# Attention scores as three float32r products, and another order of weight splits at the second feed-forward's border

## Chip, cores, metric

The kernel runs on one core of a Trainium2 chip. The metric is device time in microseconds (us). Engines: TensorE (PE; its weight loads are shown apart, as PEld), VectorE (DVE), ScalarE (ACT), GpSimd (POOL) and SyncE (SP), which issues most DMAs.

## The reference

One residual block of a streaming encoder on 256 frames of width 1024, all in float32:

```python
h = rmsnorm(x, ffn1_pre_g)
x = x + 0.5 * rmsnorm(swiglu(h, ffn1_w_in, ffn1_w_down), ffn1_post_g)
h = rmsnorm(x, mix_pre_g)
q_a, f_a, i_a, g_a, q_b, k_b, v_b, f_b, gates = split(h @ w_in)
o_a = rmsnorm(hgrn2(q_a, f_a, i_a), hg_norm_g) * silu(g_a)   # gated linear recurrence
o_b = fox_attention(q_b, k_b, v_b, f_b + bias)               # 8 heads of 128, causal
y = sigmoid(gate_A) * (o_a @ w_branch_a) + sigmoid(gate_B) * (o_b @ w_branch_b)
x = x + rmsnorm(y @ w_out, mix_post_g)
x = x + rmsnorm(mem_attention(rmsnorm(x), rmsnorm(mem)) @ w_mo, mem_post_g)
x = x + 0.5 * rmsnorm(swiglu(rmsnorm(x, ffn2_pre_g), ffn2_w_in, ffn2_w_down), ffn2_post_g)
```

Attention's logit of frame t for frame s <= t is q.k / sqrt(128) plus the sum of the log forget gates between them, and a softmax runs over s.

## The kernel before

**Precision and weights.** Most products are taken in the type float32r. Each operand is kept as two parts: the high part is the value cast to float32r, the low part is the value less the high part. A product is then three matmuls into one PSUM tile: high by high, high by low, low by high. Weights come in units of 128 x 1024 float32 (512 KB). `load_split` (line 134) loads a unit into one of four `raw` buffers (queue SP, line 141), casts it on ScalarE (line 143, `hi`) and subtracts on VectorE (line 145, `lo`), into eight buffers each; the first two units of `i_a` and of the second feed-forward go to buffers of the tag `extra` and are called `w` in the profile. Data tiles have tags as well: `m4` (21 tiles of 128 x 1024), `extra` (4 of that size). PSUM has banks `acc` (4), `mm` (2) and `tr` (2).

**Order.** A scheduler puts the instructions of each engine in a fixed order from the program's order and dependences. Two helpers steer it: `after(i)` (line 96) places a block at high priority behind the i-th matmul of a log, and `issue_after` puts an instruction behind a given one on the same engine; it is an order, not a semaphore. `hold` names, for a weight unit, the instruction pair (one of ScalarE, one of VectorE) behind which its cast and subtraction go.

**Stages.** First feed-forward, the combined projection with the recurrence, attention, gates and branches, memory attention, second feed-forward. The 256 frames are two halves of 128 (h = 0, 1). Between two stages `post` (line 384) norms a half's output and adds it to the residual `xs`: square sums of two PSUM tiles on ScalarE (line 283), `root` on ScalarE (lines 303, 304), `step` on VectorE, two residual sums on VectorE (line 404). `half` (line 599) then transposes the half in eight blocks on TensorE (line 368, four blocks to a `tr` bank), and `gain_split` writes each block's high part on ScalarE (line 358) and low part on VectorE (line 359) and notes the pair in `evicted`.

**The second feed-forward's border** (lines 1231 to 1253). The memory attention's outputs come from `mem_out` (line 1206), each in a `tr` bank. The output projection `rows_proj` of unit `mo` runs for half 0, then `post` of half 0; then 30 matmuls for half 1, and in between, behind the 20th and the 24th of them (`L_MO = 19`), the transposes of half 0. The feed-forward starts with two chunks of four units on half 0, 24 matmuls of 512 columns each, blocks of activations in rising order, then second half (transposes behind matmul `L_F2 = 36`).

**The first border** (lines 609 to 624) is alike: units of `i_a` on half 0, their second chunk's splits held behind evictions.

**Attention.** Keys and queries are projected in two groups g of four heads, scaled on VectorE (line 889), kept as float32 tiles `kb_[g]` and `qb_[g]`. `fox_scores(h)` (line 950) goes behind the 13th matmul (`F_S = 12`) of the value projection. For h = 0 each head's score is 128 x 128, in a `tr` bank; for h = 1 it is 128 x 256, in `acc` banks. Each score is one float32 matmul in the program, and two instructions in the profile. The `extra` buffers hold, one after the other, the recurrence's tiles `early` and `qf`, the gates' bias rows `brow` (loaded by SP, line 1032) and transposed probabilities.

**The start.** `WARM = 7` matmuls of ones, 128 x 128 float32 and two instructions each, run on TensorE while the first operands are loaded (lines 571, 572). Then `act_first` (line 461) takes two chunks block by block, 12 matmuls a block.

Of the kernel before, what the change touches and what calls it, by code (L numbers as in the profile page):

```python
# [12 lines left out]
F32R = mybir.dt.float32r  # L13
I32 = mybir.dt.int32
AF = mybir.ActivationFunctionType
ALU = mybir.AluOpType
AX = mybir.AxisListType

P = 128
D = 1024  # L20
T = 256
# [16 lines left out]
L_IA = 40  # L38
L_WO = 20
L_MK = 76  # L40
L_MO = 19
L_F2 = 36
L_OA = (4, 24)
F_S = 12
# [10 lines left out]

HX = T + 2 * KB

WARM = 7

X_AT = 12  # L60

# [8 lines left out]
_AT = {}  # L70
# [8 lines left out]
def block_kernel(ctx: ExitStack, tc: tile.TileContext, wts, head_in, gf_in, x_in, mem_in, memT_in, cols, rows, fbias, masks, out):  # L79
    nc = tc.nc  # L80
    V, S, G, PE = nc.vector, nc.scalar, nc.gpsimd, nc.tensor

    cp = ctx.enter_context(tc.tile_pool(name="consts", bufs=1))
    wp = ctx.enter_context(tc.tile_pool(name="weights", bufs=4))
# [7 lines left out]
    def MM(*args, **kw):  # L92
        log.append(PE.matmul(*args, **kw).ins)  # L93
# [9 lines left out]
    def nm(s):  # L103
        count[0] += 1
        return f"{s}_{count[0]}"

    def m4(shape, dt=F32, n="m"):
        return mp.tile(shape, dt, tag="m4", name=nm(n))
# [7 lines left out]
    def mm():  # L116
        return pp.tile([P, 512], F32, tag="mm", name=nm("mm"), bufs=2)

    def trp():
        return pp.tile([P, 512], F32, tag="tr", name=nm("tr"), bufs=2)  # L120
# [5 lines left out]
    evicted = []  # L126
    hold = {}
# [34 lines left out]
    def split(hi, lo, src):  # L162
        a = S.copy(hi, src)
        b = V.tensor_tensor(out=lo, in0=src, in1=hi.bitcast(F32), op=ALU.subtract)
        return a.ins, b.ins
# [124 lines left out]
    def sums_of(s, pre2=None):  # L290
# [5 lines left out]
            V.tensor_scalar(out=b, in0=s[:, 0:1], scalar1=pre2, scalar2=D * EPS, op0=ALU.mult, op1=ALU.add)  # L296
        return b

    def root(s, b, pre=None, pre2=None):

        sc = 1.0 if pre2 is None else pre2
        y, v = s1(name="y"), s1(name="v")
        S.activation(y, s[:, 1:2], AF.Abs_reciprocal_sqrt, bias=b, scale=sc)
        S.activation(v, s[:, 1:2], AF.Identity, bias=b, scale=sc)
        z = y
        if pre is not None:
            z = s1(name="z")
            S.activation(z, y, AF.Copy, scale=pre)
        return y, v, z

    def step(y, v, z):
# [25 lines left out]
    def fac_of(i, h):  # L337
        return fac[i][:, 32 * h : 32 * h + 1]
# [45 lines left out]
    def post(ps, h, grow, factor=1.0, pre=None, cuts=((0, 512), (512, 1024)), store=False):  # L384

        pre2 = None
        if pre is not None:
            pre2 = s1(name="pre2")
            V.tensor_tensor(out=pre2, in0=pre, in1=pre, op=ALU.mult)
        s = s1(2, name="ss2")  # L390
        ts = []
        for j in range(2):
            ssq(s[:, j : j + 1], ps[j])
            if j == 0:
                b = sums_of(s, pre2)
            else:
                y = root(s, b, pre, pre2)
            t = sp.tile([P, 512], F32, tag="z2", name=nm("post"), bufs=3)
            V.scalar_tensor_tensor(out=t, in0=ps[j], scalar=-factor * 16.0, in1=grow[:, j * 512 : (j + 1) * 512], op0=ALU.mult, op1=ALU.mult)  # L399
            ts.append(t)  # L400
        r = step(*y)
        for a, b in cuts:
            xh = xs[:, h, a:b]
            V.scalar_tensor_tensor(out=xh, in0=ts[a // 512][:, a % 512 : (b - 1) % 512 + 1], scalar=r, in1=xh, op0=ALU.mult, op1=ALU.add)  # L404
            if store:
                (nc.scalar if a in (320, 768) else nc.sync).dma_start(out[h * P : (h + 1) * P, a:b], xh)


    def ffn(w_in, w_dn, X, r2, n_tok, i_row, first_half, second_half=None):
# [146 lines left out]
    for kb in range(KB):  # L556
        heads.append(wp.tile([P, D], F32, tag="extra" if kb in (1, 2, 3, 4, 6) else "raw", name=nm("head"), bufs=4))
        n = HX if kb == 0 else 0
# [5 lines left out]
        if kb % 2 == 0 or kb == 1:  # L564
            a, b = ((0, 512), (512, D))[kb] if kb < 2 else (0, D)
# [4 lines left out]
    one = nc.const_aps.tensor(1.0, (P, P), F32)  # L570
    for _ in range(WARM):
        MM(wps[:, :P], one, one, start=True, stop=True)
# [26 lines left out]
    def half(X, r, h, g, *ms, into=None, act=True):  # L599

        for i, m in enumerate(ms):
            with after(m):
                to_T(X, x_blocks(h), h, g, (i,) if len(ms) == 2 else (0, 1))
        r[h] = rstd_x(x_halves(h), into, act)
# [7 lines left out]
    for h in range(2):  # L612
        m = len(log)
        for c in range(2):
            ps = mm()
            if h == 0 and c == 1:
                for i in range(4):
                    hold[_AT["i_a"] + 4 + i] = evicted[-1 if i else -3]
            u = chunk("i_a", c)
            proj_tok(ps, X2, u, h)  # L620
            iv_last = S.activation(iv[c][:, h, :], ps, AF.Copy, scale=r2[h]).ins
        if h == 0:
            half(X2, r2, 1, G_MIX, m + L_IA, into=fac_of(0, 1))
# [25 lines left out]
    for c in range(2):  # L649
        u = chunk("f_a", c)  # L650
        f, k = m4([P, 2, 4, P], n="f"), m4([P, 2, 4, P], n="k")
        for j in range(2):
            fj = heads_of(f, j)
            for i in (2 * j, 2 * j + 1):
                ps = acc()
# [10 lines left out]
    for c in range(2):  # L666
        u = chunk("q_a", c)
        q = m4([P, 2, 4, P], n="q")
        for j in range(2):
            qj = heads_of(q, j)  # L670
            z = sp.tile([P, 2, 2, P], F32, tag="z2", name=nm("z2"), bufs=3)
            for i in range(2):
                ps = acc()
# [162 lines left out]
    for c in range(3):  # L836
        u = [load_split(gf_in[4 * c + i], GF) for i in range(4)]
        n = min(GF, D - c * GF)
        for h in range(2):
            ps = mm()  # L840
# [32 lines left out]
    kb_, qb_, vb_ = [], [], []  # L873
    for c in range(2):
        for name, lst, sc in (("k_b", kb_, 1.0), ("q_b", qb_, 1.0 / math.sqrt(128.0))):
            u = chunk(name, c)
            t = m4([P, 4, T], n=name)
            m = len(log)
            for j in range(2):
                if c == 0:  # L880
                    ps = proj_col2(X2, u, (2 * j, 2 * j + 1))
                else:
                    for i, bank in enumerate((mm, trp)):
                        ps = bank()
                        proj_both(ps, X2, u, 2 * j + i)
                        added(t[:, 2 * j + i], ps)
                    ps = t[:, 2 * j : 2 * j + 2]
# [28 lines left out]
    ATs, A128s = [r.AT for r in recs], [r.A128 for r in recs]  # L916


    OA = Pair()
    for h in range(2):  # L920
        ps = [acc(), acc()]
        for hd in range(8):
            g, i = hd // 4, hd % 4
# [5 lines left out]
        r = rstd_x(ps)  # L929
# [10 lines left out]
    for g in range(2):  # L940
        t = m4([P, 4, T], n="cbm")
# [7 lines left out]

    def fox_scores(h):  # L950
        for g in range(2):
            k, q = kb_[g], qb_[g]
            ns = P * (h + 1)
            if h == 0:
                pv = trp().rearrange("p (i s) -> p i s", i=4)
                pv = [pv[:, i] for i in range(4)]
                p = sp.tile([P, 4, P], F32, tag="z2", name=nm("p0"), bufs=3)
            else:
                pv = score_psum()
                p = m4([P, 4, T], n="p1")  # L960
            mx, sm = s1(4, name="mx"), s1(4, name="sm")
            for i in range(4):
                MM(pv[i], q[:, i, h * P : (h + 1) * P], k[:, i, :ns], start=True, stop=True)
            for i in range(4):
                hd = 4 * g + i
                c1 = ct[:, h * 8 + hd : h * 8 + hd + 1]
                if h == 1:
                    V.scalar_tensor_tensor(out=p[:, i, 0:P], in0=pv[i][:, 0:P], scalar=c1, in1=cbc[:, hd], op0=ALU.add, op1=ALU.subtract)
                ds_ = slice(h * P, (h + 1) * P)
                V.scalar_tensor_tensor(out=p[:, i, ds_], in0=pv[i][:, ds_], scalar=c1, in1=cbm[g][:, i, ds_], op0=ALU.add, op1=ALU.subtract)  # L970
            V.tensor_reduce(out=mx, in_=p, axis=AX.X, op=ALU.max, negate=True)
            for i in range(4):
                S.activation(p[:, i], p[:, i], AF.Exp, bias=mx[:, i : i + 1], accum_out=sm[:, i : i + 1])
            V.reciprocal(sm, sm)
            V.tensor_tensor(out=p, in0=p, in1=bc(sm, [P, 4, ns], 2), op=ALU.mult)
            ps_[g, h] = p
# [34 lines left out]
    for c in range(2):  # L1011
        u = chunk("v_b", c)
        t = m4([P, 2, 512], n="v_b")
        for h in range(2):
            ps = mm()
# [25 lines left out]
    for h in range(2):  # L1041
        with after(m + L_OA[h]):
            to_T(OA, lambda kb: Gt[h][:, kb * P : (kb + 1) * P], h, G_HG)
    fox_pT(0, m + F_T[0])
# [38 lines left out]
    for c in range(2):  # L1083
        for name, X, zc in (("br_a", OA, c), ("br_b", OB, 2 + c)):
            u = chunk(name, c)
            for h in range(2):
                z = zs[zc][:, h]
                m = len(log)
                ps = mm()
# [21 lines left out]
    po = [[acc(), acc()], [acc(), acc()]]  # L1111
# [14 lines left out]
    for c in range(2):  # L1126
        u = chunk("mk", c)
        KM.more()
        for j in range(2):
            js = slice(2 * j, 2 * j + 2)  # L1130
            t = sp.tile([P, 2, T], F32, tag="z2", name=nm("km"), bufs=3)
            for i in range(2):
                ps = acc()
# [6 lines left out]
    for c in range(2):  # L1140
        u = chunk("mq", c)
        QM.more()
        for i in range(4):
            ps = acc()
# [3 lines left out]
            t = sp.tile([P, T], F32, tag="c1", name=nm("qm"), bufs=7)  # L1148
# [54 lines left out]
    g3 = load_row(2)  # L1203
    AO = Pair()

    def mem_out(i):
        ps = trp()
        for j in range(2):
            o = ps[:, j * T : (j + 1) * T]
            for sb in range(2):  # L1210

                n = sb * 512 + (2 * (i % 2) + j) * P
                vh = VM.h[i // 2][:, n // T, n % T : n % T + P]
                vl = VM.l[i // 2][:, n // T, n % T : n % T + P]
                MM(o, vh, pT.h[sb][:, i], start=(sb == 0), stop=False)
                MM(o, vl, pT.h[sb][:, i], start=False, stop=False)
                MM(o, vh, pT.l[sb][:, i], start=False, stop=(sb == 1))
        i2 = slice(2 * (i % 2), 2 * (i % 2) + 2)
        marks[2 + i] = split(AO.h[i // 2][:, i2], AO.l[i // 2][:, i2], ps.rearrange("p (a t) -> p a t", a=2))
# [17 lines left out]
    po = [[acc(), acc()], [acc(), acc()]]  # L1237
# [2 lines left out]
            rows_proj(po[h], AO, "mo", h, (kb,))  # L1240
    for n in range(2):
        rows_proj(po[0], AO, "mo", 0, range(3, KB), (n,))
    post(po[0], 0, g3)
    m = len(log)
    rows_proj(po[1], AO, "mo", 1, range(3, KB))
    half(X4, r4, 0, G_F2, m + L_MO, m + L_MO + 4, into=fac_of(3, 0))
    post(po[1], 1, g3)


# [95 lines left out]
```

## Time and profile before

| what | us |
|---|---|
| median of 3 runs | 787.14 |
| lowest, highest | 785.87, 789.0 |
| the profiled execution | 788.36 |
| its span, first to last instruction | 786.1 |
| VectorE busy in the span | 555.4 |
| ScalarE busy in the span | 462.8 |

A line of the profile reads: start and duration in us, engine, line of the kernel, operation, tile written <- tiles read, shape, number of merged instructions, and in brackets the engine's idle time before it with what ended it. A line of a tile's view gives the least, median and longest duration in ns, then the first and last start. A wait line gives the engine and tile that waited, what it waited for, the total in us, the number of times and the longest. A line of a window gives its borders and length, then busy time and number of instructions of each engine asked for, the granted clock, the DMA share and GB/s.

### The profile page before, as it was taken

To read this page: it belongs to the slowest core of one execution; us is meant where nothing else is said; L and a number is where in the kernel's file an instruction comes from. 1 tells how busy PE (TensorE), PEld (TensorE's weight loads), DVE (VectorE), ACT (ScalarE), POOL (GpSimd) and SP (SyncE) were. 2 spreads that over 40 slices of the span, in tenths; PEclk is the share of its full clock that TensorE was granted. 3 is DMA by queue.
4 is the path that set the end of the run, shared out by engine and by line. 5 is a ranking of instruction groups with operands and counts; after the bars stand their busy time and mean duration, and the time that the engine had idled before them with its cause. 6 is when DMAs were issued, how large, how long until landed. Compare 5 with 4: busy or idle time off the path is not lost.

```text
span 786.1 us, 12160 instructions
## 1 busy us (share of the span) xinstructions
PE 777.3 (99%) x4620; PEld 669.9 (85%) x4620; DVE 555.4 (71%) x895; ACT 462.8 (59%) x777; POOL 15.7 (2%) x39
## 2 busy tenths in 40 slices
PE   9999999999999999999999999999999999999996
PEld 7888888888888999898888888888887888888885
DVE  7766665586778899588676666885588566655563
ACT  7664544566765668467676345753667554544552
POOL 0000000000000102100000000000000000000000
PEclk9999999999999999999999999999999999999999
DMA  9665665463654546734576655465174546665431
GB/s 347 245 223 202 228 211 207 161 211 125 216 205 145 181 135 208 276 122 152 183 263 226 215 181 168 148 207 181 54 263 166 166 163 203 217 211 199 161 108 53
DMA packets 44505, 148.08 MB, mean 188 GB/s; under 512 B 5144, under 2 KB 8864, under 8 KB 44448
## 3 DMA queue, kind: packets, MB, share of 16 engines
q1 hardware_dynamic: 43168, 144.83, 53.5%
q0 software_dynamic: 848, 2.12, 1.1%
q8 instruction: 36, 0.59, 0.3%
q10 hardware_dynamic: 432, 0.37, 0.2%
q14 instruction: 21, 0.17, 0.1%
HBM read 146.24 MB, written 1.06 MB: 187 GB/s over the span
## 4 chain that ended last, share of the span: by engine, by line
PE 95%; DMA 2%; ACT 1%; DVE 1%; issue 0%; DVEq 0%; ACTq 0%
PE mm L93 43%; PE acc L93 37%; PE tr L93 13%; DMA raw<-in_wts_dram 2%; PE tr L368 1%; ACT hi L143 1%; DVE lo L145 0%; DMA head<-in_head_dram 0%; PE tr L985 0%; PE tr L426 0%; PE tr L1079 0%; PE acc L1198 0%; DVE xs L404 0%; ACT junk L283 0%; DVE post L399 0%
## 5 line engine op out<-in xcount | busy, mean ns | idle before, releaser
L145 DVE TENSOR_TENSOR lo<-raw,hi 128x1024 fp32r<-128x1024 f32 (+1 forms) x252 | 299.2, 1203 | 70.1 <-ACT hi L143 44.9
L143 ACT CAST hi<-raw 128x1024 fp32r<-128x1024 f32 (+1 forms) x252 | 254.9, 1037 | 68.0 <-PE mm L93 33.4
L93 PE MATMUL mm<-hi,hlT 128*128 128x512 f32 (+1 forms) x480 | 143.8, 379 | 0.0
L93 PE MATMUL acc<-hi,act 128*128 128x512 f32 x352 | 111.2, 390 | 0.0
L93 PEld LDWEIGHTS mm<-hi,hlT 128*128 128x128 f32 x480 | 88.1, 188 | 14.6 <-DVE hlT L359 0.3
L93 PE MATMUL mm<-hlT,hi 128*128 128x512 f32 (+1 forms) x432 | 99.5, 360 | 0.0
L93 PE MATMUL mm<-lo,hlT 128*128 128x512 f32 (+1 forms) x240 | 89.5, 378 | 0.0
L93 PEld LDWEIGHTS mm<-hlT,hi 128*128 128x128 f32 x432 | 75.5, 189 | 10.6
L93 PEld LDWEIGHTS acc<-hi,act 128*128 128x128 f32 x352 | 66.2, 188 | 13.4
L93 PE MATMUL tr<-hlT,hi 128*128 128x512 f32 x288 | 72.1, 392 | 0.0
L93 PE MATMUL acc<-lo,act 128*128 128x512 f32 x176 | 68.8, 391 | 0.0
L93 PE MATMUL acc<-hlT,hi 128*128 128x512 f32 x272 | 68.4, 393 | 0.0
L93 PE MATMUL mm<-hlT,lo 128*128 128x256 f32 x368 | 60.9, 283 | 0.0
L93 PEld LDWEIGHTS tr<-hlT,hi 128*128 128x128 f32 x288 | 51.8, 189 | 9.3
L93 PEld LDWEIGHTS acc<-hlT,hi 128*128 128x128 f32 x272 | 48.9, 189 | 8.8
L93 PEld LDWEIGHTS mm<-hlT,lo 128*128 128x128 f32 x368 | 53.7, 190 | 3.0
L93 PEld LDWEIGHTS mm<-lo,hlT 128*128 128x128 f32 x240 | 45.0, 188 | 7.0
L215 ACT COPY plo<-mm 128x256 f32<-128x256 f32 x38 | 14.1, 372 | 55.0 <-PE mm L93 55.0
L93 PEld LDWEIGHTS tr<-hlT,lo 128*128 128x128 f32 x288 | 39.3, 190 | 2.8
L93 PE MATMUL tr<-hlT,lo 128*128 128x256 f32 x288 | 40.2, 282 | 0.0
L93 PEld LDWEIGHTS acc<-hlT,lo 128*128 128x128 f32 x272 | 37.3, 190 | 2.7
L93 PE MATMUL acc<-hlT,lo 128*128 128x256 f32 x272 | 38.6, 283 | 0.0
(245 smaller groups left out, 1002.1 us busy)
## 6 DMA issues: line engine op xcount, KB each, us to landing
raw<-in_wts_dram SPq DMA_DIRECT2D x247, 512.0 KB, 4.5
raw<-in_gf_dram SPq DMA_DIRECT2D x12, 344.0 KB, 3.9
head<-in_head_dram SPq DMA_DIRECT2D x7, 392.0 KB, 6.6
grow<-in_rows_dram SPq DMA_DIRECT2D x4, 512.0 KB, 6.9
xs<-in_x_dram SPq DMA_DIRECT2D x2, 512.0 KB, 7.7
cbm<-cd POOLq DMA_DIRECT2D x2, 512.0 KB, 8.4
brow<-in_rows_dram SPq DMA_DIRECT2D x4, 256.0 KB, 4.5
memT<-in_memT_dram SPq DMA_DIRECT2D x2, 512.0 KB, 5.8
```

What stands on the lines that cost most here:

```text
L93: log.append(PE.matmul(*args, **kw).ins)
L143: S.copy(h, r)
L145: V.tensor_tensor(out=l, in0=r, in1=h.bitcast(F32), op=ALU.subtract)
L215: S.copy(lo, ps[:, T:])
L368: PE.transpose(ps[:, j * P : (j + 1) * P], src(kb), ident)
```

## The change

The border: the transposes of half 0 go four matmuls earlier; the splits of units 4, 6 and 7 of the second feed-forward are put behind `post`'s last `root` instruction and last residual sum of half 0, behind the eviction of block 3, and behind that of block 7 (unit 5 follows in program order). The third memory output uses an `mm` bank. At the first border one unit's split is held two evictions longer. One more warm-up matmul. Attention: keys and queries of each group are cast and subtracted in two pieces each (`split`, lines 162 to 165), high parts into `extra` buffers and low parts into `m4` tiles, and each score is three float32r matmuls.

```diff
-L_MO = 19
+L_MO = 15
...
-WARM = 7
+WARM = 8
...
+    rooted = []
+
     def root(s, b, pre=None, pre2=None):
...
-        S.activation(v, s[:, 1:2], AF.Identity, bias=b, scale=sc)
+        last = S.activation(v, s[:, 1:2], AF.Identity, bias=b, scale=sc).ins
...
+        rooted.append(last)
         return y, v, z
...
-            V.scalar_tensor_tensor(out=xh, in0=ts[a // 512][:, a % 512 : (b - 1) % 512 + 1], scalar=r, in1=xh, op0=ALU.mult, op1=ALU.add)
+            summed = V.scalar_tensor_tensor(out=xh, in0=ts[a // 512][:, a % 512 : (b - 1) % 512 + 1], scalar=r, in1=xh, op0=ALU.mult, op1=ALU.add)
...
+        return rooted[-1], summed.ins
...
                 for i in range(4):
-                    hold[_AT["i_a"] + 4 + i] = evicted[-1 if i else -3]
+                    hold[_AT["i_a"] + 4 + i] = evicted[-1]
...
+    kq = [[], []]
+    for g in range(2):
+        for t in (kb_[g], qb_[g]):
+            high = wp.tile([P, D], F32R, tag="extra", name=nm("qh"), bufs=4).rearrange("p (i t) -> p i t", i=4)
+            low = m4([P, 4, T], F32R, n="ql")
+            for j in range(2):
+                i2 = slice(2 * j, 2 * j + 2)
+                split(high[:, i2], low[:, i2], t[:, i2])
+            kq[g].append((high, low))
...
-            k, q = kb_[g], qb_[g]
+            (kh, kl), (qh, ql) = kq[g]
...
             for i in range(4):
-                MM(pv[i], q[:, i, h * P : (h + 1) * P], k[:, i, :ns], start=True, stop=True)
+                ts = slice(h * P, (h + 1) * P)
+                for n, (q, k) in enumerate(((qh, kh), (qh, kl), (ql, kh))):
+                    MM(pv[i], q[:, i, ts], k[:, i, :ns], start=(n == 0), stop=(n == 2))
...
-        ps = trp()
+        ps = mm() if i == 2 else trp()
...
-    post(po[0], 0, g3)
+
+    hold[_AT["f2_in"] + 4] = post(po[0], 0, g3)
     m = len(log)
     rows_proj(po[1], AO, "mo", 1, range(3, KB))
     half(X4, r4, 0, G_F2, m + L_MO, m + L_MO + 4, into=fac_of(3, 0))
+    hold[_AT["f2_in"] + 6] = evicted[-5]
+    hold[_AT["f2_in"] + 7] = evicted[-1]
     post(po[1], 1, g3)
```

## The prediction

> **What bounds the kernel now.** The first page comes first: how long TensorE is busy, and who stands beside it.
>
> ```profile
> PE 777.3 (99%) x4620; PEld 669.9 (85%) x4620; DVE 555.4 (71%) x895; ACT 462.8 (59%) x777; POOL 15.7 (2%) x39
> ```
>
> TensorE is busy for 777.3 us, 99% of the span. So the time can only change by (a) the length of matmuls that are exchanged, (b) the few waits of TensorE, or (c) a new wait. The table of waits, TensorE alone, is the second view:
>
> ```profile
> PE mm L93 <- ACT hlT L358: 0.4, 1, 0.4
> PE mm L93 <- DVE hlT L359: 0.2, 1, 0.2
> ```
>
> Besides these it names only the start (0.79 and 0.57, in the rows below) and 0.2 of no known cause: some 2 us in all. But ends of matmuls are modelled, so a matmul that starts late shows only part of its delay as idle; the distance from start to start shows all. I therefore read the timeline of TensorE at the three places that the diff touches.
>
> The start:
>
> ```profile
> 0.79 3.33 PE L93 MATMUL tr<-const-float32-1.0 128*128 128x128 f32 x14 [0.79 <-PEq L1334]
> 4.69 2.08 PE L93 MATMUL acc<-hi,hlT 128*128 128x512 f32 x4 [0.57 <-ACT hi L582]
> 6.56 1.05 PE L93 MATMUL acc<-lo,hlT 128*128 128x512 f32 x2
> 7.42 1.79 PE L93 MATMUL acc<-hi,hlT 128*128 128x512 f32 x4
> 9.04 0.62 PE L93 MATMUL acc<-lo,hlT 128*128 128x512 f32 x2
> 9.51 1.07 PE L93 MATMUL acc<-hi,hlT 128*128 128x512 f32 x4
> 10.41 0.61 PE L93 MATMUL acc<-lo,hlT 128*128 128x512 f32 x2
> ```
>
> From 9.51 to 10.41 four matmuls of 512 columns take 0.90 us, 0.225 each; this is full pace. The two from 6.56 to 7.42 take 0.43 each, half pace. The first twelve take 4.82 us instead of 12 x 0.225 = 2.70, so **2.1 us are lost at the start**.
>
> The border of the second feed-forward (TensorE, a window's sum, then ScalarE, then VectorE):
>
> ```profile
> 590.79 0.60 PE L368 MATMUL tr<-ident,xs 128*128 128x128 f32 x4
> 593.99 0.62 PE L93 MATMUL mm<-w,hlT 128*128 128x512 f32 x2
> 594.82 0.50 PE L93 MATMUL mm<-w,hlT 128*128 128x512 f32 x1 [0.21 <-DVE hlT L359]
> ```
>
> ```profile
> 593.90:601.07 7.17, 6.58 (x27) 1.00 0.75 257
> ```
>
> ```profile
> 585.70 1.04 ACT L143 CAST hi<-raw 128x1024 fp32r<-128x1024 f32 x1
> 586.64 0.59 ACT L283 ACTIVATE junk<-acc 128x512 f32<-128x512 f32 x1
> 592.21 1.03 ACT L143 CAST hi<-raw 128x1024 fp32r<-128x1024 f32 x1
> 593.14 0.36 ACT L358 ACTIVATE hlT<-tr,cols_s 128x128 fp32r<-128x128 f32 x1
> ```
>
> ```profile
> 587.05 1.22 DVE L145 TENSOR_TENSOR lo<-raw,hi 128x1024 fp32r<-128x1024 f32 x1
> 589.23 1.41 DVE L404 SCALAR_TENSOR_TENSOR xs<-post,y,xs 128x512 f32<-128x512 f32 x2
> 593.27 1.23 DVE L145 TENSOR_TENSOR lo<-raw,hi 128x1024 fp32r<-128x1024 f32 x1 [0.30 <-ACT hi L143]
> 594.42 0.35 DVE L359 SCALAR_TENSOR_TENSOR hlT<-tr,cols_s,hlT 128x128 fp32r<-128x128 f32 x1
> ```
>
> The window holds 25 matmuls that start in it (two of the 27 began before) and, from 593.99 to 601.07, lasts 7.08 us; 25 x 0.225 = 5.63. **1.4 us are lost**, of which the wait table shows 0.59. Why: the first transposed block was there after 590.79, but its high part was written at 593.14 and its low part at 594.42, each right behind a weight split (L143 to 593.24, L145 to 594.50).
>
> **The change part by part.**
>
> *Border, -1.35 us.* Unit 4 of the second feed-forward (split at 585.70 and 587.05) goes behind the first half's root and residual sum, unit 6 behind the eviction of block 3, unit 7 behind that of block 7; the transposes move from the 20th to the 16th matmul of the output projection. Without unit 4, ScalarE's square sum (586.64) starts about 0.25 sooner and VectorE's path to the sum, now at 589.23, loses 1.2 us less the small steps that wait for ScalarE: about 1 us. The sum's two halves are then done near 588.9 and 589.6. The transposes move up by 4 x 0.225 = 0.9 us, to 589.9: data that would have been late by 0.1 (first half done at 589.9 now) is there. Blocks 0 to 3 go out from about 590.4 with no split between; if high and low parts of one bank alternate, a block takes 0.36 + 0.35 = 0.71, block 3 is done by 593.3, and TensorE needs it at 593.99 + 9 x 0.225 = 596. All 1.4 us should go; I take 1.35, with 0 and 1.4 as ends. The moved splits are matters of order on ScalarE and VectorE, no new semaphores. What they push: unit 4 is needed 24 matmuls after 593.99, near 599.4, and its split now ends near 591; units 6 and 7 are needed at 602 and 603.5 and end near 595 and 597. Their raw buffers come free 2 to 3 us later, so SP issues the load of unit 8 that much later; that unit is needed after 96 matmuls, 22 us after 593.99. Next late is the second half's residual sum, with its transposes at 603.79; it shares the engines with fewer splits than before.
>
> *The first border (units of i_a) and mem_out, 0.* There the split of one unit goes behind the eviction of block 7 instead of block 5.
>
> ```profile
> 191.00 2.88 PE L93 MATMUL mm<-w,hlT 128*128 128x512 f32 x12
> 196.78 3.49 DVE L145 TENSOR_TENSOR lo<-raw,hi 128x1024 fp32r<-128x1024 f32 x3
> ```
>
> That unit is needed 24 matmuls after 191.00, at 196.4. The three low parts of the units behind it end at 196.78 + 3.49 = 200.3. The work of VectorE up to there is the same, only its order differs. If the unit's low part (a third of 3.49, 1.2) came last ahead of these three, it would end near 196.8: 0.4 late for its first use. Ends 0 and +0.9, I take 0. The memory attention's third output in another bank pair removes at most a wait of the third and fourth output for banks; no wait for it stands in the table, so 0.
>
> *Warm-up, -1.3 us.* One more call is two more matmuls of 3.33 / 14 = 0.238 us, 0.48 in all; the gap before the first real matmul is 0.57, so it delays nothing. What it brings hangs on why the first matmuls run at half pace. In the rows, 3.33 us of warm-up and a gap of 0.57 did not bring full pace. It came near 8.9, some 4 us after 4.69: the four matmuls from 7.42 to 9.04 take 1.62, a little less than 4 x 0.43, and the next go at full pace. If some 4 us of unbroken work is what it takes, the longer warm-up, unbroken but for 0.1, reaches it near 5.5. The ten matmuls left of the twelve then end near 5.5 + 2.25 = 7.8 instead of 9.51, but the second block's operands stand in the way:
>
> ```profile
> 8.13 0.48 DVE L359 SCALAR_TENSOR_TENSOR hlT<-head,hlT 128x256 fp32r<-128x256 f32 x1
> ```
>
> They are whole at 8.61, and the block's third matmul would ask for them near 8.2. Counted from there, the block starts as if at 8.61 - 2 x 0.225 = 8.16 instead of 9.51. That leaves 1.3 to 1.4. Ends: 0 and 2.1 (all that was lost). I take 1.3, by the nearest row, the 4 us. The granted clock of the profile, 1.00 here, does not show this slow pace.
>
> The Trainium skill, "TensorE: Matmul & The Clock Gate", Part 1, says that the array runs at half clock until a free-running window of about 3.4 us was busy. The half pace agrees with the rows. By that rule the gain depends on where the windows fall in a run, from nothing to all of it, which is the first rival.
>
> *Scores.* Before, each of 16 float32 scores is two instructions. After, three float32r products.
>
> ```profile
> L93 PEld LDWEIGHTS acc<-qf,early x192: 106/109/113, 268.2 to 294.8; 128*32 128x32 f32 x192
> L93 PEld LDWEIGHTS tr<-k_b,q_b x16: 187/191/192, 344.4 to 348.0; 128*128 128x128 f32 x16
> 318.60 1.11 PE L93 MATMUL tr<-hlT,lo 128*128 128x256 f32 x8
> 319.55 2.00 PE L93 MATMUL mm<-hlT,hi 128*128 128x512 f32 x8
> 345.54 1.03 PE L93 MATMUL acc<-k_b,q_b 128*128 128x256 f32 x4
> 346.40 0.38 PE L93 MATMUL tr<-k_b,q_b 128*128 128x128 f32 x2
> 347.06 1.28 PE L93 MATMUL tr<-k_b,q_b 128*128 128x128 f32 x10
> 348.17 1.89 PE L93 MATMUL acc<-k_b,q_b 128*128 128x256 f32 x8
> ```
>
> 256 columns, float32: (346.40 - 345.54) / 4 = 0.215 an instruction, 0.43 a score. float32r: (319.55 - 318.60) / 8 = 0.119, three are 0.357. Eight scores: 8 x (0.357 - 0.43) = **-0.6 us**. 128 columns, float32: (348.17 - 347.06) / 10 = 0.111, 0.222 a score. No float32r matmul under 256 columns is in the trace. From below: half of 0.119, 0.06 each, makes 8 x (0.18 - 0.222) = -0.3. From above: no gain from the narrow type at this width, 0.222 each, makes 8 x (0.666 - 0.222) = +3.6. Between them: every matmul loads its own weights, and a load of 128 columns lasts 191 ns where one of 32 lasts 109, so 0.85 ns a column, 0.11 us for 128. A matmul of 128 columns can then hardly follow another faster than about 0.11, which is also the pace of the float32 rows here. I take it: 8 x (0.333 - 0.222) = **+0.9 us**. Both widths: +0.3.
>
> The Trainium skill, the same page, "Back-to-back issue gap", gives about 81 ns a matmul for sustained matmuls of 128 columns with their loads. By it the narrow scores would cost 8 x (0.243 - 0.222) = +0.2 instead of +0.9 and the sum would be lower by 0.7; no row here shows it.
>
> *The parts' making, 0.* Four tensors, two pieces each: eight copies on ScalarE and eight subtractions on VectorE.
>
> ```profile
> L163 ACT CAST hT<-km x4: 616/622/684, 497.6 to 517.1; 128x512 fp32r<-128x512 f32 x4
> L164 DVE TENSOR_TENSOR lT<-km,hT x4: 680/680/692, 498.3 to 518.1; 128x512 fp32r<-128x512 f32 x4
> 341.70 0.90 SPq L1032 DMA_DIRECT2D brow<-in_rows_dram  x1
> 320.00:330.00 10.00, 10.00 (x57) 8.73 (x56) 7.02 (x11) 5.04 (x8) 1.22 (x2) 1.00 0.61 226
> 361.12 23.95 SPq L141 DMA_DIRECT2D raw<-in_wts_dram  x12
> 339.59 0.42 DVE L889 SCALAR_TENSOR_TENSOR q_b<-q_b,row 128x256 f32<-128x256 f32 x1
> 345.84 1.41 DVE L931 SCALAR_TENSOR_TENSOR G<-acc,rstd,G 128x512 f32<-128x512 f32 x2
> ```
>
> 5.0 us of ScalarE and 5.4 of VectorE. The last queries are whole at 340.0, so their parts are due near 341.3, or 342.5 behind one weight split; the scores' first weight loads begin at 344.4 (the 13th matmul of the value projection). Cover: about 2 us. If it goes, TensorE stands until the part is there, with the rest of the value projection queued behind the scores. The keys and the first group's queries are whole earlier, and find engines with room: from 320 to 330, VectorE 7.02 and ScalarE 5.04 us of ten. The high parts take the buffers that the gate bias rows use: the first bias load, issued by SP at 341.70, now waits for the first scores to end, until about 349. Behind it in SP's queue stand weight loads, but the next is not issued before 361.12 anyway, when a raw buffer comes free. Cover: 11 us.
>
> **Sum.** -1.35 - 1.3 + 0.3 = -2.35 us against the profiled execution, 788.36 us (span 786.1 and 2.3 around it), so 786.0. That execution lies 1.2 above the median, 787.14; the forecast for the median is 787.14 - 2.35 = **784.8 us**.
>
> **The rivals.**
> 1. *The start gains nothing* (the pace changes at its own moments). For: runs of one kernel differ by 3.1 us, 785.87 to 789.0. Against: the 4 us of the rows. -1.05: 786.1.
> 2. *The narrow products cost as much as float32*, slower than before. For: nothing in the trace has float32r under 256 columns, so nothing shows its gain there. Against: one type, one instruction each. Place: the eight first-half scores, 344.7 on. -2.35 - 0.9 + 3.6 = +0.35: 787.5, and 788.8 where the start gains nothing too. From 0.21 us a product on (0.15 without the start) the whole change loses.
> 3. *TensorE waits for the parts.* For: VectorE is in the norm chain of the recurrence's output until 345.84 + 1.41 = 347.3. Against: 2 us of cover. If the last low part comes behind that chain, up to 3 us from 344.4: -2.35 + 3 = +0.65, 787.8. With rival 2, or if the 5.4 us of subtractions then push the next weights' low parts behind their use, +4 and more: above 791.
> 4. *The border's wait only moves* to the second half's transposes: -1.0, 786.1.
> 5. *All at the good ends:* -1.4 - 2.1 - 0.6 - 0.3 = -4.4, 782.7.
>
> **How the numbers follow.** Forecast 0.30; rivals 1 and 4 together 0.26; rival 2 0.12; rival 3 0.15, half of that above 791; rival 5 0.17. A measurement of this kernel can tell about 0.5%, 3.9 us, from no change: faster means under 783.2, slower over 791.1. Faster 0.18 (rival 5 and a little), slower 0.11 (half of rival 3, and rivals 2 and 3 together), the rest, 0.71, within. The range: 782.0 at the low end (rival 5 with the spread of runs), 789.8 at the high end (rival 2 without the start, plus 1 us).
>
> **What would show it.** Right: in the changed profile the wait rows of L358 and L359 are gone and the 25 matmuls of the border take 5.7 us; the start's twelve matmuls take about 3.4; scores on 256 columns step by 0.119, on 128 by 0.11. Wrong: narrow steps near 0.22, a wait of TensorE on L163 or L164 near 345, a TensorE idle behind a raw load near 369 to 385, or the start unchanged.

## The result, and the profile after

| | us |
|---|---|
| before, median (lowest to highest) | 787.14 (785.49 to 789.0) |
| after, median (lowest to highest) | 789.02 (788.35 to 789.7) |
| ratio, 95% interval | 1.0025 [1.0017, 1.0032] |
| profiled execution after, its span | 789.41, 787.1 |

The change makes the kernel slower by 1.9 us, the difference of the medians, where 2.35 us of gain were forecast. Each engine's share of the span hardly moves, so the page does not say why:

```profile
PE 777.3 (99%) x4638; PEld 669.6 (85%) x4638; DVE 561.1 (71%) x903; ACT 466.9 (59%) x785; POOL 19.3 (2%) x39
```

What says it is a ledger of the two executions: the same instruction of TensorE looked up in both traces. Before, first products of the start's next chunk, a row behind the first border, the first score, the second matmul behind the scores, the transposes of half 1 at the second border:

```profile
28.55 1.07 PE L93 MATMUL mm<-hi,hlT 128*128 128x512 f32 x4
257.73 1.12 PE L93 MATMUL acc<-hlT,lo 128*128 128x256 f32 x8
344.67 0.38 PE L93 MATMUL tr<-k_b,q_b 128*128 128x128 f32 x2
350.13 0.63 PE L93 MATMUL mm<-hi,hlT 128*128 128x512 f32 x2
603.79 1.03 PE L368 MATMUL tr<-ident,xs 128*128 128x128 f32 x8
```

After (596.11 is the second feed-forward's first matmul, which stood at 593.99):

```profile
27.49 1.07 PE L93 MATMUL mm<-hi,hlT 128*128 128x512 f32 x4
258.85 1.11 PE L93 MATMUL acc<-hlT,lo 128*128 128x256 f32 x8
345.55 0.22 PE L93 MATMUL tr<-qh,qh 128*128 128x128 f32 x1
352.28 0.62 PE L93 MATMUL mm<-hi,hlT 128*128 128x512 f32 x2
596.11 2.88 PE L93 MATMUL mm<-w,hlT 128*128 128x512 f32 x12
604.72 1.03 PE L372 MATMUL tr<-ident,xs 128*128 128x128 f32 x8
```

Subtract row by row. At 28 us the changed kernel is 1.06 early, and at the first border's first matmul it still is (189.95 against 191.00); at 258 it is 1.12 late, so **2.2 us are lost in between**, and of what the diff touches only the first border lies there. The scores take 352.28 - 345.55 = 6.73 instead of 350.13 - 344.67 = 5.46: **1.27 lost**. The second border, from its first matmul to the transposes of half 1, takes 8.61 instead of 603.79 - 593.99 = 9.80: **1.19 gained**. The other stretches differ by 0.25 or less. At 604.72 the lag is 0.93, and the spans differ by 1.0. The medians differ by 0.9 more: the profiled execution of before, with a bad start of its own (below), lies 1.2 above its median, that of after 0.4.

TensorE's waits after, but for the 0.8 ahead of its first instruction:

```profile
PE acc L93 <- DVE G L947: 0.7, 1, 0.7
PE mm L93 <- DVE hlT L363: 0.5, 1, 0.5
PE acc L93 <- ACT hlT L362: 0.4, 1, 0.4
PE mm L93 <- ACT hlT L362: 0.3, 1, 0.3
```

L362 and L363 are the evictions that were L358 and L359. Their `mm` rows look like those of before, but they have changed place: they now belong to the first border, and at the second none is left; the `acc` row of L362 is the start's. The row of `G`, the norm of the recurrence's output, is new.

**The first border.** ScalarE there before, then after (in brackets: idle time and what ended it):

```profile
199.09 1.06 ACT L143 CAST hi<-raw 128x1024 fp32r<-128x1024 f32 x1
201.11 0.37 ACT L358 ACTIVATE hlT<-tr,cols_s 128x128 fp32r<-128x128 f32 x1
```

```profile
201.19 1.05 ACT L143 CAST hi<-raw 128x1024 fp32r<-128x1024 f32 x1 [2.47 <-DMA raw<-in_wts_dram]
202.14 0.36 ACT L362 ACTIVATE hlT<-tr,cols_s 128x128 fp32r<-128x128 f32 x1
```

ScalarE stands for 2.47 us, to 201.19, with a weight cast at the head of its queue, and that cast waits for a load. The transposes of half 1 are issued from 199.64 on (200.48 before). In kernel 6 below, where no cast stands ahead of it, the first eviction begins 0.63 us after them (199.54, 200.17); here that would be near 200.3, and it begins at 202.14, behind the cast. The chain of waits of the changed kernel's stage says why the load is late:

```profile
194.61 1.23 DVE lo L145
...
195.85 5.31 DMA raw<-in_wts_dram
```

A raw buffer comes free at the low part's end, 195.84, and SP issues the next load at 195.85; before, the same queue began at 194.52. That is 1.3 us. The load also took longer: 5.31 us, landing at 201.17, where it took 3.2 before and landed at 197.75. Two more loads follow it after 1.1 and 2.3 us (196.99, 198.13); before, the next came 3.5 us later, at 198.03. That they slow each other is an inference, which no run tests. TensorE then gets its blocks late:

```profile
202.56 0.73 PE L93 MATMUL mm<-w,hlT 128*128 128x512 f32 x2 [0.26 <-ACT hlT L362]
203.82 1.30 PE L93 MATMUL mm<-w,hlT 128*128 128x512 f32 x3 [0.53 <-DVE hlT L363]
```

**The scores.** Their pace is the forecast one (the first score on 256 columns, then the first and last of four narrow products in a row):

```profile
346.51 0.39 PE L93 MATMUL acc<-qh,qh 128*128 128x256 f32 x1 [0.74 <-DVE G L947]
...
349.22 0.28 PE L93 MATMUL tr<-qh,qh 128*128 128x128 f32 x1
...
349.56 0.28 PE L93 MATMUL tr<-qh,qh 128*128 128x128 f32 x1
```

(349.56 - 349.22) / 3 = 0.113 us a step. What is new is the wait of 0.74 at 346.51, for an accumulator that the recurrence's output holds until VectorE has normed it (`G`). VectorE at that place after, and then GpSimd after:

```profile
339.83 0.85 DVE L894 SCALAR_TENSOR_TENSOR q_b<-q_b,row 128x256 f32<-128x256 f32 x1
340.74 1.52 DVE L145 TENSOR_TENSOR lo<-raw,hi 128x1024 fp32r<-128x1024 f32 x1
343.75 0.68 DVE L164 TENSOR_TENSOR ql<-q_b,qh 128x512 fp32r<-128x512 f32 x1
345.71 1.41 DVE L947 SCALAR_TENSOR_TENSOR G<-acc,rstd,G 128x512 f32<-128x512 f32 x2
```

```profile
332.14 0.56 POOL L958 DMA_DIRECT2D cbm<-cd  x1 [13.75 <-DVE ql L164]
336.75 6.00 POOL L961 TENSOR_SCALAR_AFFINE_SELECT cbm<-cbm 128x512 f32<-128x512 f32 x4 [2.43 <-DMA cbm<-cd]
```

Before:

```profile
318.60 1.22 POOL L945 TENSOR_SCALAR_AFFINE_SELECT cbm<-cbm 128x512 f32<-128x512 f32 x2 [6.47 <-DMA cbm<-cd]
342.72 1.41 DVE L931 SCALAR_TENSOR_TENSOR G<-acc,rstd,G 128x512 f32<-128x512 f32 x2
```

Before, the first norm was over at 344.13, half a us ahead of the first score. After, it starts behind the first score. The low parts stand in front of it (0.68 for the last), and GpSimd's mask tiles (`cbm`, tag `m4` like the low parts) were held for 13.75 us behind a low part, so that their four selects run some 18 us later than before, beside the last work of VectorE ahead of the norm. Instructions there last longer: 0.85 instead of 0.42 for the scaling of the queries, 1.52 instead of 1.22 for a weight's low part.

### The profile page after: what moved, and what is told of

It reads as the page before. It is cut to its first block, busy times and chain, and to the rows that moved or that the text cites. A ratio compares the mean times of both kernels' runs of the same rounds, so it can differ in the third digit from the quotient of the medians.

```text
span 787.1 us, 12206 instructions
## 1 busy us (share of the span) xinstructions
PE 777.3 (99%) x4638; PEld 669.6 (85%) x4638; DVE 561.1 (71%) x903; ACT 466.9 (59%) x785; POOL 19.3 (2%) x39
## 3 DMA queue, kind: packets, MB, share of 16 engines
q0 software_dynamic: 848, 2.12, 1.0%
HBM read 146.24 MB, written 1.06 MB: 187 GB/s over the span
## 4 chain that ended last, share of the span: by engine, by line
PE 95%; DVE 1%; DMA 1%; ACT 1%; issue 1%; SPq 0%; DVEq 0%; ACTq 0%
PE mm L93 41%; PE acc L93 38%; PE tr L93 13%; PE tr L372 1%; DMA raw<-in_wts_dram 1%; DMA head<-in_head_dram 1%; DVE lo L145 0%; PE tr L1003 0%; ACT hi L143 0%; PE tr L431 0%; ACT hlT L362 0%; PE tr L1097 0%; PE acc L1216 0%; ACT junk L283 0%; DVE xs L408 0%
```

## The experiments

Each kernel is the one before with the edit that its diff shows. The medians of before beside which they ran are 786.54 (first four), 786.54 (next four) and 786.37 us (last four). Line numbers shift by a few lines between kernels. Gains and losses are worked out from the ratios; the differences of the medians lie within some 0.2 us of them, and each ratio's interval reaches some 0.7 us to either side.

**1 to 4: the four parts alone.**

```diff
-WARM = 7
+WARM = 8
```

> The kernel before with one more warm-up matmul, nothing else. The profiled execution of the changed kernel gained 1.05 us at the start (27.66 against 28.71 at the same matmul). Theory W1: the half pace at the start lasts differently long in each execution of the kernel before, and the execution that was profiled before had lost much (788.36, 1.2 over its median), so the median gains only 0.2 to 0.4 us (ratio 0.9995 to 0.9997) and the spread of runs shrinks from 3.5 to under 2 us. Rival W2: the 1.05 us are gained in every execution, ratio 0.9987.

786.48 us, ratio 1.0001 [0.9992, 1.001]: nothing, where the prediction had 1.3.

```diff
-                    hold[_AT["i_a"] + 4 + i] = evicted[-1 if i else -3]
+                    hold[_AT["i_a"] + 4 + i] = evicted[-1]
```

> The kernel before with only the split of the fifth unit of i_a held behind the last eviction instead of the third last. Theory T: TensorE waits at the transposes of the second half's blocks (about 2.2 us, ratio 1.0028), because the raw buffer comes free later, the next load lands later, and the cast that waits for it stands in ScalarE's queue ahead of the evictions of the second half. Rival T0 (the prediction): nothing, ratio 1.000. Rival T1: the unit's own low part is late, at most 0.9 us, ratio 1.001, with the wait at the first half's second chunk.

788.52 us, ratio 1.0023 [1.0014, 1.0032]: this one index costs 1.8 us by itself. Its ScalarE shows the same stall:

```profile
201.20 1.05 ACT L143 CAST hi<-raw 128x1024 fp32r<-128x1024 f32 x1 [2.23 <-DMA raw<-in_wts_dram]
```

```diff
-L_MO = 19
+L_MO = 15
...
-        ps = trp()
+        ps = mm() if i == 2 else trp()
...
+    hold[_AT["f2_in"] + 4] = post(po[0], 0, g3)
...
+    hold[_AT["f2_in"] + 6] = evicted[-5]
+    hold[_AT["f2_in"] + 7] = evicted[-1]
```

> The kernel before with only the second border's edits (transposes four matmuls earlier, units 4, 6 and 7 held, third memory output in the other bank pair). If the 1.2 us that the two traces show there are real in every run: -1.2 us, ratio 0.9985. If the wait only moves: 0.

785.35 us, ratio 0.9987 [0.9979, 0.9996]: a gain of 1.0 us.

```diff
+            high = wp.tile([P, D], F32R, tag="extra", name=nm("qh"), bufs=4).rearrange("p (i t) -> p i t", i=4)
+            low = m4([P, 4, T], F32R, n="ql")
...
-                MM(pv[i], q[:, i, h * P : (h + 1) * P], k[:, i, :ns], start=True, stop=True)
+                for n, (q, k) in enumerate(((qh, kh), (qh, kl), (ql, kh))):
+                    MM(pv[i], q[:, i, ts], k[:, i, :ns], start=(n == 0), stop=(n == 2))
```

> The kernel before with only keys and queries split and the scores as three float32r products. Theory S: +1.25 us (ratio 1.0016), of which 0.3 is the matmuls' pace (48 at 0.115 us against 32 at 0.111 and 0.215) and 0.95 a wait of TensorE for the accumulators that the recurrence's output holds until VectorE has normed it, late behind the low parts. Rival S2: the pace alone, +0.3 (ratio 1.0004), the wait being an accident of the whole change.

787.86 us, ratio 1.0017 [1.0008, 1.0025]: a loss of 1.3. The trace agrees: first score and second matmul behind the scores,

```profile
342.77 0.22 PE L93 MATMUL tr<-qh,qh 128*128 128x128 f32 x1
...
349.49 0.39 PE L93 MATMUL mm<-hi,hlT 128*128 128x512 f32 x1
```

6.72 us for the stage, 5.46 before, with the same wait of 0.74 for the norm. The four parts add up within the noise: 0 + 1.8 - 1.0 + 1.3 = +2.1, and the whole change measured +1.9.

**5: all but the first border.** The whole change with the line of the second diff left as it was.

> The changed kernel with the first border's one hold taken back. From the parts measured alone (second border -1.2, scores +1.3, warm-up 0): +0.1 us against the kernel before, ratio 1.000 (0.9992 to 1.001), about 2 us faster than the whole change. If the parts do not add up, the loss at the first border belongs to the whole change and the ratio stays near 1.002.

787.48 us, ratio 1.0010 [1.0001, 1.0019]: at the upper end of what was expected, and 0.5 us above the sum of the single parts. Against the whole change's 1.0025 the one index is worth some 1.2 us here.

**6: the first border with the stalled casts out of the way.** The index of the change, and also the casts and subtractions of the next weights (units 0 to 3 of `f_a`) held behind the last eviction of half 1:

```diff
+                    hold[_AT["i_a"] + 4 + i] = evicted[-1]
...
             half(X2, r2, 1, G_MIX, m + L_IA, into=fac_of(0, 1))
+            for i in range(4):
+                hold[_AT["f_a"] + i] = evicted[-1]
```

> The kernel with only the first border's hold, and with it the casts and subtractions of the next four units (f_a) held behind the last eviction of the second half. Theory T (a cast that waits for its load stands ahead of the evictions in ScalarE's queue): the waits of TensorE on the evictions at 202 to 205 go, time back to the kernel before, ratio 1.000 (at most 1.0005). Theory T1 (the unit's own low part comes late at 195.4): TensorE's 0.2 to 0.3 us there stays, and if T1 were the whole cause the ratio would stay at 1.0023.

786.44 us, ratio 0.9999 [0.999, 1.0008]: the loss is gone. The load is issued as late as in the changed kernel, and lands at 200.29, later than before by 2.5 us; what differs is the place of the cast in ScalarE's order and of the subtraction behind it in VectorE's. SP's queue, the evictions, the second half's matmuls, the casts:

```profile
195.71 18.41 SPq L141 DMA_DIRECT2D raw<-in_wts_dram  x9
...
200.17 2.38 ACT L358 ACTIVATE hlT<-tr,cols_s 128x128 fp32r<-128x128 f32 x6 [0.45 <-PE tr L368]
...
202.03 2.88 PE L93 MATMUL mm<-w,hlT 128*128 128x512 f32 x12
...
203.52 2.01 ACT L143 CAST hi<-raw 128x1024 fp32r<-128x1024 f32 x2
```

SP's queue begins at 195.71, later than before by 1.2 us, as in the change. The twelve matmuls at 202.03 run without a gap. Nor does the added hold gain anything here that would hide a loss: this kernel is 1.2 us ahead of the one before at 28 us, and 1.1 ahead at 258.

**7 and 8: where the scores' wait comes from.** Both have the scores of the fourth part. In 7 the parts are made behind the mask tiles' loads and selects in the program; in 8 behind the norm of the recurrence's output, but still ahead of the masks.

```diff
     for g in range(2):
         t = m4([P, 4, T], n="cbm")
...
         cbm.append(t)
+    kq = [[], []]
+    for g in range(2):
+        for t in (kb_[g], qb_[g]):
```

> Only the scores' change, with the making of the parts put in program order behind the recurrence's norm and the loads and masks of the log-gate tiles. Theory S (the accumulators wait for the norm, which stands behind the low parts on VectorE; the log-gate tiles wait for m4 buffers of the low parts and their masks on GpSimd then run beside VectorE and stretch it): TensorE's wait on G goes or shrinks to under 0.3, the four masks run near 319 to 322 again, ratio 1.0004 (0.9996 to 1.001). Rival: TensorE now waits for the parts themselves (L163 or L164) and the ratio stays at 1.0017 or more.

787.29 us, ratio 1.0008 [0.9999, 1.0017].

```diff
+    kq = [[], []]
+    for g in range(2):
+        for t in (kb_[g], qb_[g]):
...
     ct = s1(16, name="ct")
```

> As the run with the parts last, but the parts stand behind the recurrence's norm only, ahead of the loads of the log-gate tiles. If the norm's place in VectorE's order is the cause, this is as good as that run (ratio 1.0004). If the buffers and the late masks on GpSimd are the cause, the masks still run beside VectorE after 330 and the wait on G stays (1.0017).

787.94 us, ratio 1.0017 [1.0008, 1.0027]: no better than the fourth experiment. Kernel 7, the scores, a mask pair and the scaling of the queries:

```profile
343.04 0.22 PE L93 MATMUL tr<-qh,qh 128*128 128x128 f32 x1
343.53 0.39 PE L93 MATMUL acc<-qh,qh 128*128 128x256 f32 x1 [0.27 <-DVE G L931]
349.29 0.40 PE L93 MATMUL mm<-hi,hlT 128*128 128x512 f32 x1
317.56 1.22 POOL L945 TENSOR_SCALAR_AFFINE_SELECT cbm<-cbm 128x512 f32<-128x512 f32 x2 [6.83 <-DMA cbm<-cd]
337.98 0.42 DVE L889 SCALAR_TENSOR_TENSOR q_b<-q_b,row 128x256 f32<-128x256 f32 x1
```

Kernel 8:

```profile
334.82 5.71 POOL L956 TENSOR_SCALAR_AFFINE_SELECT cbm<-cbm 128x512 f32<-128x512 f32 x4 [2.72 <-DMA cbm<-cd]
337.61 0.85 DVE L889 SCALAR_TENSOR_TENSOR q_b<-q_b,row 128x256 f32<-128x256 f32 x1
344.16 0.39 PE L93 MATMUL acc<-qh,qh 128*128 128x256 f32 x1 [0.62 <-DVE G L931]
```

With the masks early (7) VectorE's 0.42 is back, the wait falls from 0.74 to 0.27 and the stage takes 6.25 us. With the parts behind the norm but the masks late (8), VectorE's 0.85 stays and so does most of the wait, 0.62; the stage takes 6.61 (343.32 to 349.93). So of the 0.74 the masks' lateness is worth 0.35 and the place of the subtractions ahead of the norm 0.12: it is the tiles of `m4`, claimed by the low parts ahead of the masks, more than that place, that lengthens the wait. The 0.27 that is left in 7 was not taken apart. The two times lie 0.7 us apart and their intervals overlap, so this split rests on one trace each.

**9 and 10: what gains at the second border.** The holds alone, and `L_MO = 15` alone.

```diff
+    hold[_AT["f2_in"] + 4] = post(po[0], 0, g3)
...
+    hold[_AT["f2_in"] + 6] = evicted[-5]
+    hold[_AT["f2_in"] + 7] = evicted[-1]
```

> The kernel before with only the three holds of the second feed-forward's border (unit 4 behind half 0's post, unit 6 behind the eviction of block 3, unit 7 behind that of block 7). The transposes stay behind the 20th matmul. Theory: the splits ahead of the evictions are the whole cost there, so this alone gains what the whole border gained, 1.2 us: ratio 0.9985, TensorE's wait rows for the evictions of that border gone. Rival: the gain needs the earlier transposes: half of it or less, ratio 0.9993 or more.

785.6 us, ratio 0.9989 [0.998, 0.9998].

```diff
-L_MO = 19
+L_MO = 15
```

> The kernel before with only the transposes of half 0 at the second border moved from behind the 20th to behind the 16th matmul. Theory: the weight splits still stand ahead of the evictions and of the residual sum, so nothing is gained: ratio 1.000 (0.9995 to 1.001), and TensorE may wait up to 0.9 us for the residual sum. Rival: the place of the transposes is what gains: ratio 0.9985.

786.3 us, ratio 0.9999 [0.9989, 1.0008]. The stage in the two traces, holds alone first:

```profile
592.94 2.89 PE L93 MATMUL mm<-w,hlT 128*128 128x512 f32 x12
601.83 1.03 PE L371 MATMUL tr<-ident,xs 128*128 128x128 f32 x8
```

```profile
592.47 2.46 PE L93 MATMUL mm<-w,hlT 128*128 128x512 f32 x8
601.84 1.03 PE L368 MATMUL tr<-ident,xs 128*128 128x128 f32 x8
```

8.89 and 9.37 us, against 9.80 before and 8.61 with both. The stage differs between executions, though: in the seven traces of kernels whose second border is that of before it takes 8.95 to 9.80, in the six with the holds 8.61 to 8.89. The 9.37 lies among the first, and its ratio is 1: that the earlier transposes gain anything is not shown. The holds bring 0.9 in this trace and by their ratio.

**11 and 12: put together.** All parts, with the mendings of 6 and 7; and the second border with the eighth warm-up matmul.

```diff
-WARM = 7
+WARM = 8
...
+            for i in range(4):
+                hold[_AT["f_a"] + i] = evicted[-1]
...
         cbm.append(t)
+    kq = [[], []]
```

> The whole change, with two things mended: the casts of the first four units of f_a go behind the last eviction of the first border's second half, and the keys' and queries' parts are made behind the mask tiles' loads and masks. If the parts add up as measured one by one: second border -1.2, first border 0 (held) , warm-up 0, scores +0.75, in all -0.45 us: ratio 0.9994 (0.9985 to 1.0005). Rival, that the parts touch each other (splits moved at one place move the loads of the next): a ratio above 1.001.

786.62 us, ratio 1.0006 [0.9997, 1.0015]: 1 us above the sum of the parts, just above the expected range, and no better than the kernel before.

```diff
-L_MO = 19
+L_MO = 15
...
-WARM = 7
+WARM = 8
```

> The kernel before with the second border's edits and the eighth warm-up matmul, the two parts that lost nothing alone. By the sum of the single parts -1.2 us: ratio 0.9985 (0.998 to 0.9992). If the warm-up gains its forecast 1.3 us after all: 0.997.

785.52 us, ratio 0.999 [0.9981, 0.9999]: the second border's gain and nothing from the warm-up. Kernels 3, 9 and 12 are the best; the gain that the change holds is about 1 us. Whether the mended whole truly loses a further microsecond stays open: its trace has the border (593.07 to 601.75) and the scores (342.99 to 349.25) at the lengths of the single parts, and a sum of parts with such intervals is not sure to a microsecond.

## Why the prediction was wrong

**The step that failed** is "The first border (units of i_a) and mem_out, 0." Its ends were 0 and +0.9; it cost 2.2 in the trace and 1.8 alone (experiment 2). The step asked when the moved unit is needed, and by that question it was nearly right: experiment 6 makes the same move at no measurable cost. It did not ask what the moved split frees. The split ends a raw buffer's use; SP's next load goes with it (194.52 to 195.85) and lands 3.4 us later, and the cast that waits for this load stands ahead of the half's evictions in ScalarE's fixed order. Where the prediction traced exactly this, at the second border ("SP issues the load of unit 8 that much later"), it came out free. The Trainium skill, "TensorE: Matmul & The Clock Gate", "Architectural detail: the array is 16× 32×32, not 1× 128×128", calls ScalarE's queue a strict FIFO; the 2.47 us of standing, the last 0.9 of them with a block to evict, agree.

**Scores, +0.3: pace right, wait missed.** The products take 352.05 - 346.51 = 5.54 us for 47 steps, 0.118 each, and the narrow step is 0.113 where 0.11 was taken; rival 2 is out. From the first product to 346.51 pass 0.96 us instead of one step, so 0.84 is waiting; the rest of the 1.27, 0.43, is near the +0.3. The wait is rival 3, with the right place (VectorE's norm chain) but two things off: TensorE waits for an accumulator and not for a part, and the price is under 1 us, not 3. "Cover: about 2 us" counted the time to the parts' own use. The cover that gave way belonged to the norm: 344.67 - 344.13 = 0.5 us. The Trainium skill's 81 ns a matmul for 128 columns ("Back-to-back issue gap" of the page above) does not hold for these: 0.113 was measured.

**Warm-up, -1.3: nothing, rival 1.** The trace did move: the first twelve matmuls take 3.46 us (4.60 to 8.06), as forecast. But so do those of kernels that keep seven warm-up matmuls, and one with eight took longer. Second border only (seven), then warm-up only (eight):

```profile
4.46 1.20 PE L93 MATMUL acc<-hi,hlT 128*128 128x512 f32 x4 [0.39 <-ACT hi L586]
7.81 1.44 PE L93 MATMUL acc<-hi,hlT 128*128 128x512 f32 x4 [0.20 <-ACT hlT L361]
```

```profile
4.34 1.97 PE L93 MATMUL acc<-hi,hlT 128*128 128x512 f32 x4
8.31 1.45 PE L93 MATMUL acc<-hi,hlT 128*128 128x512 f32 x4 [0.15 <-ACT hlT L358]
```

3.35 us with seven, 3.97 with eight. Over all other traces the twelve take 3.14 to 3.84 us with seven (eight kernels) and 3.24 to 3.97 with eight (five kernels). The 4.82 of the profiled execution before is in none of them: it was that execution's own bad start, and it lay 1.2 above the median. Subtracting this loss from the median counted as gain what the other executions do not lose.

**Second border, -1.35: right.** 1.19 in the trace, 1.0 alone. The wait rows are gone, the 25 matmuls take 5.88 us (596.11 to 601.99) instead of 7.08, and the splits ahead of the evictions were most of it (0.9), as argued. Part of the 9.80 was this execution's own: the other six with that border took 8.95 to 9.77. Rival 4 did not come. **The bias rows**, moved behind the scores, cost nothing: from 352.28 to 596.11 the lag does not grow (2.15, then 2.12).

**The sum**, with sizes measured alone: -1.0 + 1.8 + 0 + 1.3 = +2.1 instead of -2.35. 789.02 lies inside the range, and that is luck: its high end stood for rival 2 with an unchanged start, and rival 2 did not come. The mechanism that spent most was in no rival.

## What to carry to other kernels

When a step is moved later, ask what buffer it frees and which load waits for that buffer, then look where the consumer of that load stands in an engine's fixed order: it may stand ahead of work that was ready. New tiles from a shared pool go in front of everyone who asks after them in the program, so look at those next in line, even on an engine that is 2% busy. Don't subtract a loss seen in one execution from a median before other executions show it as well.

## What was not expected of the hardware

Four selects on GpSimd took 6.00 us beside a busy VectorE, where two pairs took 1.22 each before, and VectorE's own instructions there grew, from 0.42 to 0.85 and from 1.22 to 1.52, though not all of them. The Trainium skill, "SBUF — State Buffer", "Who interferes with whom", says that a VectorE instruction with two inputs in SBUF contends with a GpSimd instruction that reads SBUF; these rows agree.

The pace of the first matmuls changes at a moment that differs between executions: of the two traces above, the first four matmuls take 1.03 us in one (4.46 to 5.49) and 1.80 in the other (4.34 to 6.14), where the next two then take 0.47. The free-running window that the prediction cites fits this; no run here shows the window itself.
